# Attention in pairs of heads: both heads' scores on two row halves, values stationary, probabilities scaled on ScalarE

## The chip, the cores and the metric

One NeuronCore of one Trainium2 chip runs the whole program. The metric is device time in microseconds, from runs of the whole kernel: 657.15 us is the median of three (657.02 to 658.48).

## The reference

One layer on 256 tokens of width 1024, all in float32: a feed-forward block, a mixer of a convolution branch and an attention branch, and a second feed-forward block. What matters here is the attention. There are 16 heads of 64, and with 256 tokens there is one block of 256 keys, so that only the causal part of the head's own block is left:

```
s_own = jnp.einsum('bhqd,bhkd->bhqk', q_c, k_own).astype(jnp.float32) * scale
s_own = jnp.where(k_pos[None, :] <= q_pos[:, None], s_own, NEG_INF)
...
p = jax.nn.softmax(logits, axis=-1)
...
o = (jnp.einsum('bhqk,bhkd->bhqd', p_own, v_own.astype(jnp.float32))
...
y_b = moba_attention(q, k, v) @ w_attn_proj
```

## The kernel before

Every large product is made of three: a float32 weight is split into a high part (`hi`, rounded on ScalarE, L91) and a low part (`lo`, on VectorE or GpSimd, L93), and the activations likewise. `gemm` (L97) goes through the weights in pieces of two k-tiles of 128 rows by 512 columns; a piece is loaded (SyncE's queue), split, and used by twelve matmuls of 512 columns (two token tiles, two k-tiles, L133 to L135). Five pieces can be in flight.

The attention is a generator of small steps. While the keys, queries and values of heads 8 to 15 and then the four gate products run, `gemm` takes steps from it after each piece: `SIDE` of them, 1.25 in the first three products (12 pieces) and 1.5 in the four gate products (16 pieces). Beside it runs the convolution, in steps of two 255-column multiply-adds on VectorE (L317), by `PUMP` per piece. A scheduler orders each engine's instructions by a simulated timeline, so that the order in the trace is near that of the source, but not the same.

`score(h)` makes the scores of one head for two token tiles t (the first sees 128 keys, the second 256), as two matmuls with 64 rows, rows 0 to 63 for even heads and 64 to 127 for odd ones (L419). VectorE adds the mask and takes the maximum (L430), negates it (L434), and ScalarE takes Exp with row sums (L437). `value(h)`, one score later, transposes the three 128x128 blocks of probabilities (L448), copies them to SBUF (L452), and multiplies with the transposed probabilities as the stationary operand and 64 columns of v moving (L459). VectorE takes the reciprocals of the row sums (L465) and scales the output with them (L466). After each four heads the output is transposed by `to_T` (L472, L178) and split into its parts `oh` and `ol` (L187, L188) for the product with `w_attn`.

A float32 matmul stands in the trace as two passes of a weight load and a matmul; a transpose and a product of the split weights as one. PSUM tiles `tr` have three buffers.

Of the kernel before, what the change touches and what calls it, by code (L numbers as in the profile page):

```python
# [17 lines left out]
P = 128  # L18
S = 256
# [10 lines left out]

# columns of the packed small parameters
C_GM, C_G2, C_QN, C_KN = 0, 8, 16, 17
C_CB, C_LG, C_LB, C_DW = 18, 26, 34, 42
C_ALL = C_DW + KD * TAPS

KP = 2            # k-tiles of 128 rows in one piece of weights
RAW_BUFS, HI_BUFS, LO_BUFS = 5, 5, 5
B8_BUFS = 13
SIDE = 1.25, 1.5   # steps of the attention per piece of weights
PUMP = 3, 3.5, 3, 8   # steps of the convolution per piece of weights  # L40
WARM = 8          # products that only bring the tensor engine to its full clock
LATER = 2         # pieces of the next product before the transposes of the last


class Build:
# [9 lines left out]

# [1 line left out]
    def big(self, name, dt=F32):  # L57
# [7 lines left out]

# [1 line left out]
    def pump(self, n=1):  # L67
# [19 lines left out]

# [1 line left out]
    def split(self, raw, hi, lo, pool_lo):  # L89
# [7 lines left out]
    def gemm(self, w, c, n, kt, ah, al, pump=0, pool=0.0, first=False, split_k=None,  # L97
             side=None, before=None):
        """acc[t][128 tokens, n] = A @ W[:, chunk c]; ah/al give the [128, 128]
        stationary parts of A^T for (k, t)."""  # L100
        nc = self.nc
# [45 lines left out]

# [1 line left out]
    def rsqrt_mean(self, ss, n, width):  # L149
        """(ss / n + eps) ** -0.5 for a [128, width] tile"""  # L150
        nc = self.nc
        ms = self.tmp.tile([P, width], F32, tag=f"ms{width}", name="ms", bufs=2)
        nc.vector.tensor_scalar(ms, ss, 1.0 / n, EPS, ALU.mult, ALU.add)  # L153
        r = self.tmp.tile([P, width], F32, tag=f"rs{width}", name="rs", bufs=4)
        nc.gpsimd.tensor_tensor(r, ms, self.neghalf[:, :width], ALU.pow)  # L155
        return r

    def sum_squares(self, x, ss, t, c):
        """ss[:, c, t] = sum of squares of x[t][:, chunk c]"""
        junk = self.tmp.tile([P, CH], F32, tag="junk", name="junk", bufs=2)  # L160
        self.nc.scalar.activation(
            junk, x[:, t * D + c * CH : t * D + (c + 1) * CH], AF.Square,
            accum_out=ss[:, c * 2 + t : c * 2 + t + 1],
        )
# [6 lines left out]
    def to_T(self, src, hi, lo, k0, gain=None):  # L171
        """src(t, j) -> [128 tokens, 128 columns] for two column tiles j; writes
        the transposed tiles k0, k0 + 1 of hi/lo ([128, k, 256])."""
        nc = self.nc
        ps = self.tr()
        for j in range(2):
            for t in range(2):
                nc.tensor.transpose(  # L178
                    ps[:, j * S + t * P : j * S + (t + 1) * P], src(t, j), self.ident
                )  # L180
        return self.split_T(ps, hi, lo, k0, 2, gain)
# [28 lines left out]

# [1 line left out]
    def ffn(self, wgu, wd, hT, rstd_of, x, emit, tail=None, before=None, after=None):  # L212
        """emit(t, c, psum) takes the down products of chunk c."""
        nc = self.nc
# [68 lines left out]
    def residual_T(self, x_new, ss, hi, lo, gain):  # L283
        """after chunk c of the new residual stream: statistics, transposed parts"""
        def transp(c):
# [11 lines left out]

# [1 line left out]
    def conv(self, uT, tiles):  # L299
        """replaces tile c of uT ([channels, tokens]) by its convolution"""  # L300
        nc = self.nc
# [65 lines left out]

# [1 line left out]
    def head_norm(self, acc, rstd, c, dst, gain):  # L369
        """normalises the 8 heads of chunk c and writes them transposed"""  # L370
        nc = self.nc
# [36 lines left out]
    def attention(self, qT, kT, v, oh, ol):  # L408
        nc = self.nc
        scale = HD ** -0.5  # L410
        sums = {}
        probs = {}

        def score(h):
            b, r = h // 2, slice((h % 2) * HD, (h % 2 + 1) * HD)
            sums[h] = self.tmp.tile([P, 2], F32, tag="sums", name="sums", bufs=3)
            ps = self.tr()
            for t in range(2):
                nc.tensor.matmul(  # L419
                    ps[:, t * P : t * P + (t + 1) * P],  # L420
                    qT[r, b * S + t * P : b * S + (t + 1) * P],
                    kT[r, b * S : b * S + (t + 1) * P],
                    start=True, stop=True,
                )
            pr = self.tmp.tile([P, 3 * P], F32, tag="pr", name="pr", bufs=3)
            mx = self.tmp.tile([P, 2], F32, tag="mx", name="mx", bufs=3)
            nb = self.tmp.tile([P, 2], F32, tag="nb", name="nb", bufs=3)
            for t in range(2):
                sl = slice(t * P, t * P + (t + 1) * P)
                nc.vector.tensor_tensor_reduce(  # L430
                    pr[:, sl], ps[:, sl], self.mask[:, (1 - t) * P :], 1.0, NEG,
                    ALU.add, ALU.max, mx[:, t : t + 1],
                )
            self.anchor = nc.vector.tensor_scalar(nb, mx, -scale, None, ALU.mult)  # L434
            for t in range(2):
                sl = slice(t * P, t * P + (t + 1) * P)
                nc.scalar.activation(  # L437
                    pr[:, sl], pr[:, sl], AF.Exp, bias=nb[:, t : t + 1], scale=scale,
                    accum_out=sums[h][:, t : t + 1],
                )  # L440
            probs[h] = pr

        def value(h):
            pr = probs.pop(h)
            g = h // 4
            ps = self.tr()
            for i in range(3):
                nc.tensor.transpose(  # L448
                    ps[:, i * P : (i + 1) * P], pr[:, i * P : (i + 1) * P], self.ident
                )  # L450
            pT = self.tmp.tile([P, 3 * P], F32, tag="pT", name="pT", bufs=2)
            nc.scalar.copy(pT, ps[:, : 3 * P])  # L452
            if h % 4 == 0:
                self.on = self.tmp.tile([P, CH], F32, tag="on", name="on", bufs=2)
            on = self.on
            for t in range(2):
                o = ps[:, 3 * P + t * HD : 3 * P + (t + 1) * HD]
                for kt in range(t + 1):
                    nc.tensor.matmul(  # L459
                        o, pT[:, (t + kt) * P : (t + kt + 1) * P],  # L460
                        v[:, kt * D + h * HD : kt * D + (h + 1) * HD],
                        start=kt == 0, stop=kt == t,
                    )
            rs = self.tmp.tile([P, 2], F32, tag="rsum", name="rsum", bufs=2)
            nc.vector.reciprocal(rs, sums.pop(h))  # L465
            nc.vector.tensor_tensor(  # L466
                on.rearrange("p (t h d) -> p t h d", t=2, d=HD)[:, :, h % 4, :],
                ps[:, 3 * P :].rearrange("p (t d) -> p t d", d=HD),
                rs.unsqueeze(2).to_broadcast((P, 2, HD)), ALU.mult,
            )  # L470
            if h % 4 == 3:
                self.last_att = self.to_T(  # L472
                    lambda t, q: on[:, t * S + q * P : t * S + (q + 1) * P], oh, ol, g * 2
                )

        for h in range(H + 1):
            if h < H:
                score(h)
                yield 1
            if h > 0:  # L480
                value(h - 1)
                yield 1

# [1 line left out]
    def run(self):  # L485
# [31 lines left out]
        def start(k0):  # L517
            """the part of x^T that goes with the weights from k-tile k0 on"""
            if k0 == 0:
# [34 lines left out]
        def rstd_x():  # L554
            """statistics of x by products of its squares with ones"""
            sums = self.tr()
# [14 lines left out]

        # FFN 1
        x1 = self.big("x1")
# [15 lines left out]

        # mixer  # L590
        w_in = w_of("w_in", KD)
# [117 lines left out]

        # FFN 2  # L710
        out = io["out"]
# [17 lines left out]
def _pack(cols, kt):  # L729
    """list of [K, n] column chunks -> one flat array, each chunk [128, k, n]"""  # L730
    return np.concatenate(
# [66 lines left out]
```

## Time and profile before

| what | value |
|---|---|
| median of 3 runs | 657.15 us (657.02 to 658.48) |
| span of the profiled execution | 655.4 us |
| TensorE (PE) busy | 645.9 us, 99% |
| VectorE (DVE) busy | 417.5 us, 64% |
| ScalarE (ACT) busy | 332.9 us, 51% |
| GpSimd (POOL) busy | 133.3 us, 20% |
| attention's first scores, last values | 282.0 us, 406 us from the span's start |

The span is that of one profiled execution, from its first to its last instruction. A busy time is the union of an engine's instructions; matmuls overlap one another, so that PE's says only that something was in flight. Start times in the timeline say more. The idle time of an engine counts only where it is the one that others wait for.

### The profile page before, as it was taken

The numbers are of one execution on the slowest core, as the hardware profiler recorded it, in microseconds if no ns is written. First come the engines' busy times: TensorE is split into PE (matmuls) and PEld (weight loads), VectorE is DVE, ScalarE is ACT, GpSimd is POOL, SyncE is SP. The second block draws the span as 40 slices with busy tenths as digits, with TensorE's granted clock in tenths as the row PEclk, the third lists the DMA queues.
The fourth block names the chain that finished last, engine by engine and source line by source line (L and its number), as shares of the span: only waits on it lengthen the run. The fifth ranks groups of instructions, "written<-read, shape, count | busy, mean of one in ns | idle before, by whom it ended". The sixth has DMA issues, their size and how long they took to land.

```text
span 655.4 us, 8241 instructions
## 1 busy us (share of the span) xinstructions
PE 645.9 (99%) x3004; PEld 528.7 (81%) x3004; DVE 417.5 (64%) x692; ACT 332.9 (51%) x476; POOL 133.3 (20%) x80
## 2 busy tenths in 40 slices
PE   7999999999999999999999999999999999999997
PEld 5788888888888888877778778788888888888886
DVE  6765645464622599999999685675754646455541
ACT  6544455353545546666465374943745535444330
POOL 6200000000035667947545300000000000000000
PEclk8999999999999999999999999999999999999999
DMA  8864655556554545435333442265645555546630
GB/s 279 324 211 161 212 172 194 192 160 225 175 192 148 210 176 194 162 137 174 131 137 135 154 135 92 92 230 174 207 161 197 188 198 170 199 161 191 216 124 32
DMA packets 33000, 114.98 MB, mean 175 GB/s; under 512 B 3648, under 2 KB 5056, under 8 KB 32960
## 3 DMA queue, kind: packets, MB, share of 16 engines
q1 hardware_dynamic: 32960, 114.46, 51.3%
q8 instruction: 23, 0.38, 0.2%
q14 instruction: 17, 0.14, 0.1%
HBM read 113.40 MB, written 1.05 MB: 175 GB/s over the span
## 4 chain that ended last, share of the span: by engine, by line
PE 84%; DVE 9%; ACT 3%; issue 1%; DMA 1%; SPq 0%; DVEq 0%; ACTq 0%
PE acc L133 26%; PE acc L134 26%; PE acc L135 26%; DVE cv L317 5%; PE tr L178 2%; DVE lo L93 1%; DMA raw<-w1gu 1%; PE tr L419 1%; PE tr L459 1%; DVE hxn L385 1%; ACT gate L670 1%; DVE nb L434 1%; ACT z L359 1%; PE tr L448 1%; DVE pr L430 0%
## 5 line engine op out<-in xcount | busy, mean ns | idle before, releaser
L91 ACT CAST hi<-raw 128x1024 fp32r<-128x1024 f32 (+1 forms) x216 | 223.1, 1037 | 241.7 <-PE acc L135 214.3
L93 DVE TENSOR_TENSOR lo<-raw,hi 128x1024 fp32r<-128x1024 f32 (+1 forms) x174 | 215.9, 1245 | 183.3 <-ACT hi L91 178.3
L93 POOL TENSOR_TENSOR lo<-raw,hi 128x1024 fp32r<-128x1024 f32 x42 | 101.5, 2434 | 220.8 <-ACT hi L91 220.7
L317 DVE SCALAR_TENSOR_TENSOR cv<-uT,cst,cv 128x255 f32<-128x255 f32 (+14 forms) x240 | 95.2, 463 | 0.0
L134 PE MATMUL acc<-lo,h1h 128*128 128x512 f32 x224 | 88.0, 393 | 0.0
L135 PE MATMUL acc<-hi,h1l 128*128 128x512 f32 x224 | 87.8, 395 | 0.0
L133 PE MATMUL acc<-hi,h1h 128*128 128x512 f32 x224 | 87.7, 397 | 0.0
L133 PE MATMUL acc<-hi,hTh 128*128 128x512 f32 x176 | 68.8, 397 | 2.2 <-ACT hi L91 2.2
L134 PE MATMUL acc<-lo,hTh 128*128 128x512 f32 x176 | 69.9, 397 | 0.6 <-DVE lo L93 0.6
L135 PE MATMUL acc<-hi,hTl 128*128 128x512 f32 x176 | 69.2, 394 | 0.0
L133 PE MATMUL acc<-hi,h2h 128*128 128x512 f32 x176 | 69.1, 393 | 0.0
L133 PE MATMUL acc<-hi,aTh 128*128 128x512 f32 x176 | 68.7, 391 | 0.0
L135 PE MATMUL acc<-hi,aTl 128*128 128x512 f32 x176 | 68.5, 389 | 0.0
L134 PE MATMUL acc<-lo,aTh 128*128 128x512 f32 x176 | 68.5, 389 | 0.0
L134 PE MATMUL acc<-lo,h2h 128*128 128x512 f32 x176 | 68.4, 390 | 0.0
L135 PE MATMUL acc<-hi,h2l 128*128 128x512 f32 x176 | 67.2, 390 | 0.0
L133 PEld LDWEIGHTS acc<-hi,h1h 128*128 128x128 f32 x224 | 42.1, 188 | 10.2 <-issue 1.7
L135 PEld LDWEIGHTS acc<-hi,h1l 128*128 128x128 f32 x224 | 42.1, 188 | 9.0 <-issue 0.7
L134 PEld LDWEIGHTS acc<-lo,h1h 128*128 128x128 f32 x224 | 42.1, 188 | 8.5 <-issue 0.3
L133 PEld LDWEIGHTS acc<-hi,hTh 128*128 128x128 f32 x176 | 33.4, 191 | 9.6 <-ACT hi L91 2.9
L134 PEld LDWEIGHTS acc<-lo,hTh 128*128 128x128 f32 x176 | 33.4, 190 | 8.8 <-DVE lo L93 2.1
L155 POOL TENSOR_TENSOR rs<-ms,neghalf 128x8 f32<-128x8 f32 (+2 forms) x13 | 17.3, 1332 | 111.5 <-DVE ms L153 111.3
(133 smaller groups left out, 800.9 us busy)
## 6 DMA issues: line engine op xcount, KB each, us to landing
raw<-w_in SPq DMA_DIRECT2D x56, 512.0 KB, 3.2
raw<-w2gu SPq DMA_DIRECT2D x44, 512.0 KB, 4.2
raw<-w1gu SPq DMA_DIRECT2D x43, 512.0 KB, 5.2
raw<-w1d SPq DMA_DIRECT2D x22, 512.0 KB, 4.4
raw<-w2d SPq DMA_DIRECT2D x22, 512.0 KB, 4.4
raw<-w_attn SPq DMA_DIRECT2D x8, 512.0 KB, 3.2
raw<-w_conv SPq DMA_DIRECT2D x8, 512.0 KB, 3.2
raw<-w_out SPq DMA_DIRECT2D x8, 512.0 KB, 4.9
```

The lines of the kernel that those rows point to most:

```text
L91: nc.scalar.copy(hi, raw)
L93: ins = eng.tensor_tensor(lo, raw, hi.bitcast(F32), ALU.subtract)
L133: nc.tensor.matmul(o, ah(k, t), wh, start=st, stop=False)
L134: nc.tensor.matmul(o, ah(k, t), wl, start=False, stop=False)
L135: nc.tensor.matmul(o, al(k, t), wh, start=False, stop=sp)
L155: nc.gpsimd.tensor_tensor(r, ms, self.neghalf[:, :width], ALU.pow)
L178: nc.tensor.transpose(ps[:, j * S + t * P : j * S + (t + 1) * P], src(t, j), self.ident)
L317: nc.vector.scalar_tensor_tensor(o, i, w, o, ALU.mult, ALU.add)
L359: nc.scalar.activation(z[:, q * S : (q + 1) * S], ps[:, q * S : (q + 1) * S], AF.Silu, bias=cst[:, C_LB + c + q : C_LB + c + q + 1], scale ...
L385: nc.vector.tensor_tensor(xn.rearrange("p (h d) -> p h d", d=HD), x.rearrange("p (h d) -> p h d", d=HD), r.unsqueeze(2).to_broadcast((P, 8 ...
L419: nc.tensor.matmul(ps[:, t * P : t * P + (t + 1) * P], qT[r, b * S + t * P : b * S + (t + 1) * P], kT[r, b * S : b * S + (t + 1) * P], sta ...
L434: self.anchor = nc.vector.tensor_scalar(nb, mx, -scale, None, ALU.mult)
```

## The change

The generator now takes a pair of heads b (heads 2b and 2b + 1) in three steps: `score(b)`, `flip(b)` and `value(b)`. `SIDE` becomes 1.0, 1.0.

- `score` issues four matmuls, alternating between the heads and so between rows 0 to 63 and 64 to 127, into two `tr` tiles. Masking, Exp and row sums are as before, on tiles of twice the width with two buffers in place of three. The reciprocals follow at once, and ScalarE multiplies the probabilities by them in place.
- `flip` transposes the six blocks of the pair.
- `value` takes 64 columns of v as the stationary operand and moves the transposed probabilities (256 columns for the first key tile, 128 for the second). The first head's output lands on partitions 0 to 63 and the second's on 64 to 127 of one `tr` tile, already transposed, and is split into `oh` and `ol` per pair. `to_T` is no longer called for the attention.

```diff
-SIDE = 1.25, 1.5   # steps of the attention per piece of weights
+SIDE = 1.0, 1.0
...
-        def score(h):
-            b, r = h // 2, slice((h % 2) * HD, (h % 2 + 1) * HD)
...
+        def blk(q, t):
+            o = q * 3 * P + t * P
+            return slice(o, o + (t + 1) * P)
+
+        def score(b):
+            ps = [self.tr(), self.tr()]
+            for t in range(2):
+                for q in range(2):
+                    r = slice(q * HD, (q + 1) * HD)
+                    nc.tensor.matmul(
+                        ps[q][:, t * P : t * P + (t + 1) * P],
+                        qT[r, b * S + t * P : b * S + (t + 1) * P],
+                        kT[r, b * S : b * S + (t + 1) * P],
+                        start=True, stop=True,
+                    )
+            pr = self.tmp.tile([P, 6 * P], F32, tag="pr", name="pr", bufs=2)
...
+            for q in range(2):
+                for t in range(2):
+                    i = q * 2 + t
+                    nc.vector.tensor_tensor_reduce(
+                        pr[:, blk(q, t)], ps[q][:, t * P : t * P + (t + 1) * P],
+                        self.mask[:, (1 - t) * P :], 1.0, NEG,
+                        ALU.add, ALU.max, mx[:, i : i + 1],
+                    )
+            self.anchor = nc.vector.tensor_scalar(nb, mx, -scale, None, ALU.mult)
+            for q in range(2):
+                for t in range(2):
+                    i = q * 2 + t
+                    nc.scalar.activation(
+                        pr[:, blk(q, t)], pr[:, blk(q, t)], AF.Exp, bias=nb[:, i : i + 1],
+                        scale=scale, accum_out=sums[:, i : i + 1],
+                    )
+            rs = self.tmp.tile([P, 4], F32, tag="rsum", name="rsum", bufs=2)
+            nc.vector.reciprocal(rs, sums)
+            for q in range(2):
+                for t in range(2):
+                    i = q * 2 + t
+                    nc.scalar.activation(
+                        pr[:, blk(q, t)], pr[:, blk(q, t)], AF.Copy, scale=rs[:, i : i + 1]
+                    )
+            state[b] = pr
+
+        def flip(b):
+            pr = state[b]
+            pT = self.tmp.tile([P, 6 * P], F32, tag="pT", name="pT", bufs=2)
+            for q in range(2):
+                ps = self.tr()
+                for i in range(3):
+                    o = (q * 3 + i) * P
+                    nc.tensor.transpose(
+                        ps[:, i * P : (i + 1) * P], pr[:, o : o + P], self.ident
+                    )
+                nc.scalar.copy(pT[:, q * 3 * P : (q + 1) * 3 * P], ps[:, : 3 * P])
+            state[b] = pT
+
+        def value(b):
+            pT = state.pop(b)
             ps = self.tr()
...
+            for kt in range(2):
+                for q in range(2):
+                    h = b * 2 + q
+                    o = q * 3 * P + kt * 2 * P
+                    n = (2 - kt) * P
                     nc.tensor.matmul(
-                        o, pT[:, (t + kt) * P : (t + kt + 1) * P],
+                        ps[q * HD : (q + 1) * HD, kt * P : S],
                         v[:, kt * D + h * HD : kt * D + (h + 1) * HD],
-                        start=kt == 0, stop=kt == t,
+                        pT[:, o : o + n],
+                        start=kt == 0, stop=kt == 1, skip_group_check=True,
                     )
...
-            nc.vector.reciprocal(rs, sums.pop(h))
-            nc.vector.tensor_tensor(
-                on.rearrange("p (t h d) -> p t h d", t=2, d=HD)[:, :, h % 4, :],
-                ps[:, 3 * P :].rearrange("p (t d) -> p t d", d=HD),
-                rs.unsqueeze(2).to_broadcast((P, 2, HD)), ALU.mult,
-            )
-            if h % 4 == 3:
-                self.last_att = self.to_T(
-                    lambda t, q: on[:, t * S + q * P : t * S + (q + 1) * P], oh, ol, g * 2
-                )
+            self.last_att = self.split_T(ps, oh, ol, b, 1, None)
...
+        NB = H // 2
+        for b in range(NB + 1):
+            if b < NB:
+                score(b)
                 yield 1
+            if b > 0:
+                flip(b - 1)
+                yield 1
+                value(b - 1)
+                yield 1
```

## Rows read from the trace of the kernel before

**Rows 1.** The page's first part: busy time, share of the span, instructions.
```profile
PE 645.9 (99%) x3004; PEld 528.7 (81%) x3004; DVE 417.5 (64%) x692; ACT 332.9 (51%) x476; POOL 133.3 (20%) x80
```

**Rows 2.** The chain that ended last: shares of the span by engine.
```profile
PE 84%; DVE 9%; ACT 3%; issue 1%; DMA 1%; SPq 0%; DVEq 0%; ACTq 0%
```

**Rows 3.** Waits of PE, largest two kinds: us in total, times, longest us.
```profile
PE acc L133 <- ACT hi L91: 2.2, 1, 2.2
PE tr L510 <- DVE ones L515: 1.1, 1, 1.1
...
```

**Rows 4.** Timeline of PE, 281 to 283 us: start us, us, instruction.
```profile
281.72 0.39 PE L133 MATMUL acc<-hi,h1h 128*128 128x512 f32 x1
282.04 0.93 PE L419 MATMUL tr<-kT,qT 64*128 64x128 f32 x8
...
283.23 0.39 PE L134 MATMUL acc<-lo,h1h 128*128 128x512 f32 x1
```

**Rows 5.** Timeline of PE, 296 to 301 us.
```profile
296.18 0.39 PE L134 MATMUL acc<-lo,h1h 128*128 128x512 f32 x1
...
296.86 0.39 PE L134 MATMUL acc<-lo,h1h 128*128 128x512 f32 x1
297.18 0.92 PE L419 MATMUL tr<-kT,qT 64*128 64x128 f32 x4
...
298.36 0.39 PE L134 MATMUL acc<-lo,h1h 128*128 128x512 f32 x1
298.59 0.39 PE L135 MATMUL acc<-hi,h1l 128*128 128x512 f32 x1
298.82 1.45 PE L459 MATMUL tr<-v,pT 128*128 128x64 f32 x12
...
300.39 0.39 PE L134 MATMUL acc<-lo,h1h 128*128 128x512 f32 x1
```

**Rows 6.** Timeline of PE, 348 to 350 us.
```profile
348.92 0.39 PE L135 MATMUL acc<-hi,h1l 128*128 128x512 f32 x1
349.15 0.49 PE L448 MATMUL tr<-ident,pr 128*128 128x128 f32 x3
...
349.71 0.39 PE L134 MATMUL acc<-lo,h1h 128*128 128x512 f32 x1
```

**Rows 7.** Timeline of PE in short windows: starts of three of one head's passes.
```profile
344.30 0.49 PE L419 MATMUL tr<-kT,qT 64*128 64x128 f32 x2
344.41 0.59 PE L419 MATMUL tr<-kT,qT 64*128 64x256 f32 x2
344.63 0.38 PE L419 MATMUL tr<-kT,qT 64*128 64x256 f32 x1
```

**Rows 8.** Two stretches: length, busy PE PEld DVE ACT POOL, PEclk, DMA share, GB/s.
```profile
268.00:345.00 77.00, 75.91 (x375) 60.05 (x373) 77.00 (x200) 45.75 (x88) 47.21 (x22) 1.00 0.41 149
345.00:406.00 61.00, 60.83 (x317) 48.47 (x316) 46.23 (x128) 33.60 (x70) 15.38 (x8) 1.00 0.38 134
```

**Rows 9.** Groups of DVE by form: busy us, mean ns, idle before.
```profile
L434 DVE TENSOR_SCALAR nb<-mx 128x2 f32<-128x2 f32 x16 | 8.6, 537 | 0.2
...
L466 DVE TENSOR_TENSOR on<-tr,rsum 128x128 f32<-128x128 f32 x16 | 4.6, 286 | 6.3 <-PE tr L459 6.3
...
L188 DVE TENSOR_TENSOR ol<-tr,oh 128x512 fp32r<-128x512 f32 x4 | 2.7, 683 | 1.2 <-ACT oh L187 1.1
...
L465 DVE RECIPROCAL rsum<-sums 128x2 f32<-128x2 f32 x16 | 2.5, 154 | 0.9 <-ACT pr L437 0.7
```

**Rows 10.** Groups of ACT by form, 268 to 406 us.
```profile
L437 ACT ACTIVATE pr<-pr,nb 128x256 f32<-128x256 f32 x16 | 7.9, 494 | 0.0
...
L437 ACT ACTIVATE pr<-pr,nb 128x128 f32<-128x128 f32 x16 | 6.4, 401 | 29.0 <-DVE nb L434 29.0
```

**Rows 11.** Waits of ACT, 268 to 406 us: us in total, times, longest us.
```profile
ACT pr L437 <- DVE nb L434: 29.0, 10, 5.9
ACT hi L91 <- PE acc L135: 13.3, 10, 4.0
```

More of the change, by code (lines that the diff above doesn't have):

```diff
@@ L410, in attention @@
         scale = HD ** -0.5
-        sums = {}
-        probs = {}
-        def score(h):
-            b, r = h // 2, slice((h % 2) * HD, (h % 2 + 1) * HD)
-            sums[h] = self.tmp.tile([P, 2], F32, tag="sums", name="sums", bufs=3)
-            ps = self.tr()
[L418 to L423, printed above, removed]
-                )
[L425 to L432, printed above, removed]
-                )
[L434 to L458, printed above, removed]
+        state = {}
@@ new lines, in blk @@
+        def blk(q, t):
[13 more added lines that the diff above has]
+            pr = self.tmp.tile([P, 6 * P], F32, tag="pr", name="pr", bufs=2)
+            mx = self.tmp.tile([P, 4], F32, tag="mx", name="mx", bufs=2)
+            nb = self.tmp.tile([P, 4], F32, tag="nb", name="nb", bufs=2)
+            sums = self.tmp.tile([P, 4], F32, tag="sums", name="sums", bufs=2)
+            for q in range(2):
[23 more added lines that the diff above has]
+            state[b] = pr
@@ L464, in value @@
-            rs = self.tmp.tile([P, 2], F32, tag="rsum", name="rsum", bufs=2)
-            nc.vector.reciprocal(rs, sums.pop(h))
-            nc.vector.tensor_tensor(
-                on.rearrange("p (t h d) -> p t h d", t=2, d=HD)[:, :, h % 4, :],
-                ps[:, 3 * P :].rearrange("p (t d) -> p t d", d=HD),
-                rs.unsqueeze(2).to_broadcast((P, 2, HD)), ALU.mult,
-            )
-            if h % 4 == 3:
-                self.last_att = self.to_T(
-                    lambda t, q: on[:, t * S + q * P : t * S + (q + 1) * P], oh, ol, g * 2
-                )
@@ L476, in attention @@
-        for h in range(H + 1):
-            if h < H:
-                score(h)
+                        pT[:, o : o + n],
+                        start=kt == 0, stop=kt == 1, skip_group_check=True,
+                    )
+            self.last_att = self.split_T(ps, oh, ol, b, 1, None)
[3 more added lines that the diff above has]
+                score(b)
                 yield 1
-            if h > 0:
-                value(h - 1)
+            if b > 0:
+                flip(b - 1)
+                yield 1
+                value(b - 1)
```

## Prediction

> **What bounds the kernel now.** I read the page's first part, then the chain of waits, then TensorE's own waits. TensorE (PE) is busy 99% of the span [rows 1], the chain that ended last lies on it for 84% [rows 2], and its waits are small: the longest is 2.2 us at the start, and the eight kinds add up to 5.4 us [rows 3]. So an edit is worth what it takes off PE's stream, provided that no other engine then holds PE up. A busy PE row hides how dense the stream is, since its matmuls overlap; I therefore price by start times in the timeline. Two stretches of the mixer hold the attention, and in both the granted clock is 1.00 [rows 8]. VectorE (DVE) is the engine to watch: 77.00 of 77.00 us busy from 268 to 345, but 46.23 of 61.00 after that. ScalarE (ACT) is busy 45.75 and 33.60.
>
> **Prices on PE.** Large products start 0.227 us apart: 296.18 to 296.86 is three of them [rows 5]. A visit to something small costs the time from the product before it to the second product after it, less 2 x 0.227.
> - Scores of one head: 296.86 to 298.36 is 1.50, less 0.45: 1.05 us. Its four passes stream only 0.66 (0.11 for 128 columns and 0.22 for 256, twice each, [rows 7]); 0.39 is spent getting in and out of the 64-row form.
> - Scores of two heads side by side: once in this trace heads 0 and 1 happened to run next to each other, eight passes: 281.72 to 283.23 [rows 4], 1.51 less 0.45: 1.06 us. The second head, on the other 64 rows, was almost free. That is the row on which the forecast rests.
> - Values of two heads, twelve passes: 298.59 to 300.39, 1.80 less 0.45: 1.35, or 0.675 a head [rows 5].
> - Three transposes: 348.92 to 349.71, 0.79 less 0.45: 0.34, or 0.11 each [rows 6].
>
> **The change part by part.**
> - *Scores in pairs.* Before: 14 visits of one head and one of two, 14 x 1.05 + 1.06 = 15.8. After: 8 visits of two, 8 x 1.06 = 8.5. PE -7.3.
> - *Values stationary.* Before 16 x 0.675 = 10.8. After, each pair has eight passes, four on each 64-column half of the array, and moves 256 and 128 columns as the scores do. No row of before shows two column halves. Nearest is the pair of row halves: 8 x 1.06 = 8.5, PE -2.3. If the halves run one after the other, a pair streams 2 x 0.66 and pays 0.39 to get in and out: 1.71 x 8 = 13.7, PE +2.9. I take -2.3, because the same machine in the same two-pass form overlapped two halves fully; both ends go into the range.
> - *Output born transposed.* Four calls of the transposing helper go, with 16 transposes: 16 x 0.11 = 1.8. PE -1.8. The 48 transposes of probabilities stay, six together in place of three.
> - *DVE.* Gone: 16 multiplications by the reciprocals (4.6), 8 of 16 reciprocals (1.2), 8 of 16 negations (half of 8.6 = 4.3; at least 1.2 if each cost only what a reciprocal of that size does). Evictions of the low part: 4 of 512 columns (2.7) become 8 of 256; between the 0.286 of 128 columns and the 0.683 of 512 a line gives about 0.42 for 256, so 3.3, +0.6 [rows 9]. Sum -9.5 (ends -6.4 and -9.5).
> - *ACT.* 32 scalings of probabilities are new, in the forms of the Exp rows: 16 x (0.494 + 0.401) = 14.3 [rows 10]. The high part's evictions also double in count; at 0.494 each they are at most 4.0 in all.
> - *New waits.* The reciprocal on DVE now waits for four Exps of its pair; convolution products and low parts of weights are queued behind it. The scalings on ACT wait for that reciprocal; behind them are casts of weights, for which PE waits. PE's transposes wait for the scalings; large products are behind them. Cover: a pair's transposes are issued four steps after its scores, about four pieces of weights of 12 x 0.227 = 2.7 us, some 11 us, against 1.06 of scores, 1.8 each of Exp and of scaling [rows 10], and DVE's masking in between. If the cover goes, PE loses the difference. I cost this at nothing of its own.
> - *Steps.* 32 steps at 1.25 and 1.5 per piece become 24 at 1.0: both end at piece 24 of 28. The scores of heads 8 and 9 now come one piece (2.7 us) after the transposes that make their queries; four transposes (0.45) and one eviction, at up to 0.7 by the nearest row of that width [rows 9], fit in that. If not, PE waits about 1.
> - *Queues.* No DMA is added or moved, and POOL's and SP's queues keep their work.
> - *What is late next: DVE.* About half of the attention lies in the stretch where DVE has no idle time. There PE gets shorter by half of 11.4 = 5.7 and DVE by half of 9.5 = 4.7, so PE would run into DVE for 1.0 (ends 0, if DVE's backlog goes into its 14.8 us idle later, and 5.7, all of that half). I take 1.0.
>
> Sum: -7.3 - 2.3 - 1.8 + 1.0 = -10.4. The profiled span is 655.4 and the median of the runs 657.15, so 1.75 lies around the span or between executions; I keep it. 655.4 - 10.4 = 645.0, and 646.8 as time.
>
> **A rule against the change.** The scores' 1.05 us hold 0.39 that is not streaming [rows 5, 7]. The Trainium skill, "TensorEngine Tiling (Array Packing)", section Key Properties, says that changing the tiling mode drains the TensorE. By that rule the trace agrees at the scores, and the values, until now in full 128x128 form, would start to pay it too; my 1.06 a pair has it in. Were there no drain, the pair would cost 0.66 and the sum would be 3.2 lower.
>
> **The rivals.**
> 1. *Column halves don't overlap.* For it: no row of before shows them. Against: the row halves. -7.3 + 2.9 - 1.8 + 1.0 = -5.2: 652.0.
> 2. *Passes start strictly in the order written.* The change writes one head's matmul, of two passes, and then the other's; only the second pass of one would then overlap the first of the next: 0.11 + 0.11 + 0.22 + 0.22 + 0.22 = 0.88 of streaming in place of 0.66 for a pair, 0.22 more in each of 16 visits, +3.5: 650.3. Against: 281.72 to 283.23 was full overlap [rows 4]; there the source has one head's four passes before the other's, and such an order would have overlapped only 0.11 of 2 x 0.66. The Trainium skill, "TensorE: Matmul & The Clock Gate", section The mechanism, says that matmuls are strictly first in, first out and only weight loads overtake. By that rule this rival holds; the trace's one pair speaks against it.
> 3. *The pairs are broken up.* The kernel's scheduler orders instructions by its own timeline and may put transposes between a pair's scores. Then -7.3 goes: -3.1, 654.0. Against: it laid two separate heads side by side unasked [rows 4].
> 4. *ACT becomes the bound (slower).* ACT is busy 79.4 of the 138 us and waits 29.0 for the negated maxima, in ten stops of 2.9 [rows 8, 11]. After: 79.4 + 14.3 = 93.7 in 127.6, or 33.9 idle. Each pair now stops ACT twice, once for the maxima and once for the reciprocals, 16 stops. It decides at 33.9 / 16 = 2.1 us a stop. At 2.9 it overflows by 12.5, to 659.3, and with the evictions' 4.0 to 663; middle 661. For it: DVE's full stretch, through which the reciprocal must pass. Against: 13.3 us of ACT's idle time today is waiting for PE to free a buffer [rows 11], which says that casts run well ahead, and DVE is slack in the second half.
>
> **How the numbers follow.** Forecast 0.60; rival 1 0.16; rival 2 0.08; rival 3 0.04; rival 4 0.12. Faster by over 0.3% (which is about what a measurement of this kernel can tell from no change) means under 655.2: all of the first four, 0.88, less 0.02 for stalls of rival 4's kind that only cancel the gain. Of rival 4 I give 0.09 to slower and the rest to same: 0.86, 0.05, 0.09. Range: the low end is the sum without the 1.0, with PE's 1.26 us of idle time in the two stretches [rows 8] gone and 0.1 less per value visit for half-wide weights: -11.4 - 1.26 - 0.8 = -13.46: 643.7. The high end takes in rivals 1 to 3 and 1.0 of ACT's stops on rival 3: 655.0. It leaves out rival 4 and little else.
>
> **What would show it.** Right: scores in 8 groups of eight passes at about 0.86 us from first start to next product; value groups of eight passes at the same; no transposes of the attention's output; from 268 to the end of the gates some 10 us shorter, PE still 99% busy. Wrong: value groups at 1.3 or more (rival 1) or both groups near 1.1 (rival 2); scores in groups of four (rival 3); PE idle behind casts, with ACT waiting on reciprocals over 2.1 us a stop (rival 4).

## The result and the profile after

The changed kernel takes 653.47 us (median of four runs, 653.23 to 653.98) against 657.82 for the kernel before, run beside it: a ratio of 0.9939 [0.9927, 0.9952], 4.35 us or 0.6% faster. That lies inside the range, but 10.4 us were forecast. The profiled span fell from 655.4 to 652.2 us, 3.2; the profile after lost 0.75 us in its first stage, at products that the change doesn't touch, so that the change itself is worth 4.0 in the profile.

The page of the kernel after: first part, and the chain that ended last (answer to [rows 1, 2]).

```profile
PE 640.5 (98%) x2956; PEld 519.8 (80%) x2956; DVE 413.1 (63%) x664; ACT 342.6 (53%) x512; POOL 132.5 (20%) x80
...
PE 90%; DVE 3%; ACT 3%; DMA 1%; issue 1%; SPq 0%; DVEq 0%; ACTq 0%
```

PE bounds the kernel more than before (90% of the chain). What holds it up, by PE's waits of the kernel after (us in total, times, longest; answer to [rows 3]):

```profile
PE acc L133 <- ACT hi L91: 2.9, 1, 2.9
PE acc L133 <- ACT u2h L365: 1.3, 1, 1.3
PE tr L466 <- DVE ms L153: 1.2, 1, 1.2
```

The first is at the start of the kernel. The second has grown (it was 0.2), and is behind the attention: the first product with `w_conv` waits for the rounded output of the convolution branch (`u2h`). The third is in the attention, at 316.54: transposes wait for VectorE. The kernel before had about as much of that in its attention, in three stops:

```profile
PE tr L178 <- DVE on L466: 0.6, 1, 0.6
...
PE tr L397 <- DVE mx L430: 0.3, 1, 0.3
...
PE tr L178 <- DVE mx L430: 0.2, 1, 0.2
```

The rest of the gain has to be looked for in PE's stream. One pair runs there as forecast: the values of one pair and, right behind, the scores of another (PE, kernel after: start us, us, instruction; answer to [rows 4, 5]).

```profile
340.81 0.39 PE L135 MATMUL acc<-hi,h1l 128*128 128x512 f32 x1
341.13 0.87 PE L481 MATMUL tr<-pT,v 128*64 128x256 f32 x8
341.93 0.93 PE L423 MATMUL tr<-kT,qT 64*128 64x128 f32 x8
342.79 0.50 PE L133 MATMUL acc<-hi,h1h 128*128 128x512 f32 x1
343.13 0.40 PE L134 MATMUL acc<-lo,h1h 128*128 128x512 f32 x1
```

Sixteen passes go between 340.81 and 343.13, which by the prediction's measure (less 2 x 0.227) is 1.87 us for both groups, even below the 2 x 1.06 that it had. The eight value passes take 0.80 from their first start to the scores' first. The more frequent picture, in the same view:

```profile
354.68 0.40 PE L133 MATMUL acc<-hi,h1h 128*128 128x512 f32 x1
355.01 0.65 PE L481 MATMUL tr<-pT,v 128*64 128x256 f32 x2
355.58 0.92 PE L423 MATMUL tr<-kT,qT 64*128 64x128 f32 x4
356.43 0.86 PE L481 MATMUL tr<-pT,v 128*64 128x256 f32 x6
357.23 0.92 PE L423 MATMUL tr<-kT,qT 64*128 64x128 f32 x4
358.08 0.50 PE L133 MATMUL acc<-hi,h1h 128*128 128x512 f32 x1
358.41 0.40 PE L134 MATMUL acc<-lo,h1h 128*128 128x512 f32 x1
```

The same sixteen passes, but cut: the first head's first value matmul (two passes), the scores of one head (four), the other six value passes, the scores of the other head. Nothing lies beside its partner, and the array changes its form five times in place of three. From the product before to the second product after it is 3.28 us by the same measure, 1.41 more. In the whole trace only two of eight value groups are whole (341.13 and 396.68), and only two of eight pairs of scores (282.78 and 341.93), with a third partly so (306.18). Added up place by place against whole groups (waits taken out, and 0.11 for each transpose that stands between), this costs 9.2 us: 1.4 here, and 0.8 to 1.9 at six other places. It is rival 3.

### The profile page after: what moved, and what is told of

Read it like the earlier page. It is cut to its first block, busy times and chain, and to the rows that moved or that the text cites. A ratio compares the mean times of both kernels' runs of the same rounds, so it can differ in the third digit from the quotient of the medians.

```text
span 652.2 us, 8131 instructions
## 1 busy us (share of the span) xinstructions
PE 640.5 (98%) x2956; PEld 519.8 (80%) x2956; DVE 413.1 (63%) x664; ACT 342.6 (53%) x512; POOL 132.5 (20%) x80
## 3 DMA queue, kind: packets, MB, share of 16 engines
HBM read 113.40 MB, written 1.05 MB: 175 GB/s over the span
## 4 chain that ended last, share of the span: by engine, by line
PE 90%; DVE 3%; ACT 3%; DMA 1%; issue 1%; SPq 0%; DVEq 0%; ACTq 0%
PE acc L134 28%; PE acc L133 28%; PE acc L135 28%; PE tr L178 2%; PE tr L423 1%; DMA raw<-w1gu 1%; PE tr L481 1%; DVE cv L317 1%; DVE lo L93 1%; ACT hi L91 1%; PE tr L466 1%; ACT gate L686 1%; ACT pr L445 0%; DVE hxn L385 0%; PE tr L397 0%
## 5 line engine op out<-in xcount | busy, mean ns | idle before, releaser
L317 DVE SCALAR_TENSOR_TENSOR cv<-uT,cst,cv 128x255 f32<-128x255 f32 (+26 forms) x240 | 94.4, 463 | 0.1
L133 PEld LDWEIGHTS acc<-hi,h1h 128*128 128x128 f32 x224 | 42.1, 188 | 10.4 <-issue 1.3
```

Source lines behind the costliest of these rows:

```text
L133: nc.tensor.matmul(o, ah(k, t), wh, start=st, stop=False)
L317: nc.vector.scalar_tensor_tensor(o, i, w, o, ALU.mult, ALU.add)
```

## The experiments

Of the two theories on record, A says that the gain went where the groups are cut, and B that it went into ScalarE's scalings and the waits around them. Runs of the kernel before beside the experiments had medians of 657.09 to 657.56. Where I give a difference in the attention alone, PE's large products of two profiles were matched by their number, and their starts compared from just before the first scores on; by this measure the change as made is 5.3 ahead of the kernel before at the end of the `w_attn` product, and 4.0 ahead at the end of the `w_conv` product.

**One line: the second half first.** The value matmuls need the transposed probabilities of two heads, which ScalarE copies in two instructions, first head first. If the first matmul in the text needs only the first copy, the scheduler can place it, and finds something else for the time until the second copy. In `value`, the loop runs the other way here, so that the first matmul needs the copy that comes last.

```diff
             for kt in range(2):
-                for q in range(2):
+                for q in (1, 0):
```

> The changed kernel with one edit: value() issues the matmul of the second head of the pair ahead of the first one's, so that its first matmul waits for the copy of probabilities that ends last, and all four can then follow one another. Theory A (the pairs of products are broken up on TensorE, each broken pair costing 0.9 to 1.6 us, some 7.7 us in all by the timeline of the changed kernel; one score pair breaks newly, 1.0): about 6.7 us faster than the change, 646 to 648. Theory B (the gain went into waits for VectorE and ScalarE): nothing changes there, 652.5 to 654.5.

Measured: 649.41 us (648.89 to 650.92), ratio 0.9887 [0.9872, 0.9902]: 4.1 faster than the change as made, and 3.5 faster than the control below, which ran beside it. PE, kernel with the line swapped:

```profile
354.88 0.39 PE L133 MATMUL acc<-hi,h1h 128*128 128x512 f32 x1
355.20 0.87 PE L481 MATMUL tr<-pT,v 128*64 128x256 f32 x8
356.00 0.93 PE L423 MATMUL tr<-kT,qT 64*128 64x128 f32 x8
356.86 0.50 PE L134 MATMUL acc<-lo,h1h 128*128 128x512 f32 x1
```

The pair that was cut at 355.01 is whole. All eight value groups are whole now, and six of eight pairs of scores; at the end of `w_attn` PE is 9.55 ahead of the kernel before, 4.2 more than in the change. The scores and values alone got 6.4 shorter by the count above; PE's waits up to there grew from 1.5 to 3.7, mostly by a new one of 2.1 for VectorE's masking. Arithmetic and data are the same: the order of a loop of two is worth 3.5 to 4.1 us.

**The control: the same swap in the scores.** In `score`, both matmuls become ready together, so that the order should not matter.

```diff
             for t in range(2):
-                for q in range(2):
+                for q in (1, 0):
```

> Control to the first: the same swap of heads in score() alone. The products of value() stay broken as in the change. Theory A: as the change, 652.5 to 654.5. If the swap itself (and not the unbroken group) were what helps, this would be faster too.

Measured: 652.93 (652.73 to 653.63), 0.9939 [0.9924, 0.9953]: as the change, and the same value groups are cut (353.88, 367.37 and 374.12 among them). So not any reordering helps, but the one of the values.

**Whole groups without the scalings.** The row sums' division is left out of the computation here: the 32 multiplications on ScalarE are gone.

```diff
-            for q in range(2):
-                for t in range(2):
-                    i = q * 2 + t
-                    nc.scalar.activation(
-                        pr[:, blk(q, t)], pr[:, blk(q, t)], AF.Copy, scale=rs[:, i : i + 1]
-                    )
```

> The first experiment without the 32 scalings of probabilities on ScalarE (the row sums' division is left out of the computation; the reciprocals stay). It takes 14.4 us off ScalarE. Theory A: TensorE's stream is the same, within 1 us of the first experiment. Theory B (ScalarE's longer queue holds TensorE up): 3 us or more faster than the first.

Measured: 646.26 (646.2 to 646.38), 0.9836 [0.9819, 0.9852]; 3.15 below the swapped kernel. A expected at most 1, so B has a share: once the groups are whole, the scalings cost 3.2 us. Where they cost it shows in PE's waits, first with the scalings (swapped kernel), then without (the ones at the kernel's start, for splitting weights and in its last stages are left out).

```profile
PE tr L397 <- DVE mx L436: 2.1, 1, 2.1
PE acc L133 <- ACT u2h L365: 1.3, 1, 1.3
...
PE tr L423 <- ACT ynat L331: 0.8, 1, 0.8
PE tr L481 <- ACT pT L469: 0.6, 1, 0.6
```

```profile
PE tr L397 <- DVE mx L436: 0.3, 1, 0.3
PE acc L133 <- ACT u2h L365: 0.3, 1, 0.3
PE tr L328 <- ACT uT L320: 0.2, 1, 0.2
PE tr L475 <- ACT pT L463: 0.2, 1, 0.2
```

The four waits of the attention and of its end add up to 4.8 with the scalings, and the four without to 1.0. Without them PE is 11.6 ahead of the kernel before at the end of `w_attn` and 11.5 at the end of `w_conv`, so that almost nothing is given back on the way. That it is so near the prediction's sum without its 1.0 for DVE, 11.4, is in part chance: two pairs of scores are still cut here (286.18 and 335.34), and whole groups cost less than the prediction had them at.

**The end of the attention.** What is given back between the ends of `w_attn` and `w_conv` (1.4 in the change, 1.5 with the swapped line) is ScalarE's. Its stream in the kernel after, from the last rounding of the attention's output:

```profile
403.85 0.37 ACT L187 CAST oh<-tr 128x256 fp32r<-128x256 f32 x1 [4.92 <-PE tr L481]
404.24 1.28 ACT L686 ACT_TABLE_LOAD   x1
405.53 4.28 ACT L686 ACTIVATE gate<-gate 128x512 f32<-128x512 f32 x8
409.81 1.28 ACT L359 ACT_TABLE_LOAD   x1
411.11 1.93 ACT L359 ACTIVATE z<-tr,cst 128x256 f32<-128x256 f32 x4
412.92 2.00 ACT L91 CAST hi<-raw 128x1024 fp32r<-128x1024 f32 x2
414.80 1.16 ACT L365 CAST u2h<-z 128x512 fp32r<-128x512 f32 x2
```

The gates' Sigmoids, two loads of function tables, the convolution's Silus and the rounding for `w_conv` form a chain of 11.0 us behind the attention's last output. In the kernel before it took 10.2, from 407.41 to 417.64, and without the scalings 10.0, from 396.45 to 406.47; in these two, one cast of weights (1.05 us) stands ahead of `u2h`, in the change and in the swapped kernel two (2.00), and PE waits 0.2 and 0.3 in place of 1.3. An attention that ends earlier on PE meets a chain that doesn't get shorter, and gets a cast longer here. In the step that makes Silus and roundings two tiles at a time, I ordered each pair's Silus behind the rounding of the pair before:

```diff
-            nc.scalar.copy(h, z)
+            after = nc.scalar.copy(h, z)
```

> The first experiment (value halves swapped) with one edit in the convolution's last step: ScalarE makes the rounded part of one pair of tiles before the Silu of the next pair. In the change and in the first experiment ScalarE did four Silus and two weight casts ahead of it, and TensorE waited 1.3 us for the first product of w_conv; in the kernel before it alternated. If the loss of 1.4 to 1.5 us there comes from that order: about 1.4 us faster than the first experiment. If ScalarE is simply late because of the 32 scalings: no change.

Measured: 650.2 (649.82 to 652.97), 0.9901 [0.9879, 0.9922], no gain over 649.41. PE's wait for `u2h` fell from 1.3 to 0.4, and a wait of 0.9 for the rounded activations of a later product came in its place. That chain is real; this is not the way to shorten it.

**The scalings on another engine.** On VectorE (`nc.vector.tensor_scalar` in place of `nc.scalar.activation`, on the swapped kernel):

> The first experiment with the 32 scalings of probabilities on VectorE in place of ScalarE. Leaving them out gave 3.2 us (third experiment). If it is ScalarE's queue that costs those 3.2 us: 646 to 648, near the third. If any engine in the chain from scores to transposes would cost as much, or VectorE's full stretch takes it back: 649 to 652.

Measured: 667.19 (666.64 to 667.28), 1.0148 [1.0133, 1.0163]: a miss for every expectation. PE's waits:

```profile
PE tr L466 <- DVE ol L188: 7.7, 3, 3.1
```

PE can't start transposes, since no `tr` buffer is free, and the buffer waits for VectorE's `ol`. So the prediction's eye on VectorE was not empty: the scalings there turn the gain into a loss of 10. On GpSimd (`nc.gpsimd.tensor_scalar`):

> As the sixth, with the scalings on GpSimd, which was busy 62 of 138 us in the two stretches. By ScalarE's queue: near the third experiment, 646 to 648. If GpSimd's own time (0.9 us for 128x256 in the start of this kernel, some 3 us a pair) or its conflict with VectorE's small operations counts: 649 to 655.

Measured: 652.35 with a scatter of 649.92 to 656.12 over eight runs, 0.9927 [0.9903, 0.9951]: not better than ScalarE, and no more can be said.

**The scores' term alone.** The kernel before with the paired `score` only; values, division and transposes as they were; one step per piece.

```diff
-SIDE = 1.25, 1.5   # steps of the attention per piece of weights
+SIDE = 1.0, 1.0   # steps of the attention per piece of weights
...
-        def score(h):
+        def score(b):
+            ps = [self.tr(), self.tr()]
```

> The kernel before with the change's score() alone, in three steps a pair (scores of the pair, value of one head, value of the other), SIDE 1.0; values, scaling of the output and its transposes as before. With three PSUM buffers the scheduler keeps only 2 of 8 score pairs side by side here, two more are split by transposes only. By the prediction's term (-7.3 for scores in pairs): 650. By theory A (a pair costs what its pieces cost when something comes between): about 2 us faster than before or less, 655 to 657.

Measured: 658.63 (656.94 to 659.06, ten runs), 1.0015 [1.0005, 1.0025]: no gain, where the prediction's -7.3 would have given 650. Two of eight pairs run side by side, the other twelve heads alone, as two of them do at 360.09 and 361.30 with two transposes between. By the prediction's own prices that is 12 x 1.05 + 2 x 1.06 = 14.7 in place of 15.8: -1.1. Against it stands a new wait of PE, 1.9 us in one stop, for a buffer that VectorE's scaling has to leave:

```profile
PE tr L419 <- DVE on L469: 1.9, 1, 1.9
```

**Pairing in the text against pairing on PE.** The swapped kernel, but with the scores of each head written on their own (and `SIDE` 1.25, 1.5, so that the steps end at the same piece):

```diff
-        def score(b):
-            ps = [self.tr(), self.tr()]
+        def score(h):
+            b, q = h // 2, h % 2
+            ps = self.tr()
...
-                score(b)
+                score(2 * b)
+                yield 1
+                score(2 * b + 1)
```

> The first experiment with score() per head again (two tiles of the kernel before in place of one of a pair, SIDE 1.25, 1.5), values and scaling as in the first experiment. The scheduler lays 5 of 8 pairs of scores side by side by itself, against 6 of 8 in the first experiment. Theory A (only what is adjacent on TensorE counts, not how the source pairs it): within 1.5 us of the first experiment, 649 to 651. If pairing in the source is what brings the 7.3 us: about 656.

Measured: 650.18 (649.24 to 650.66), 0.989 [0.9875, 0.9905], within 0.8 of the paired text. The scheduler laid five of the eight pairs side by side unasked. So it's not how the matmuls are written that counts, but what stands next to them on PE.

**A fourth `tr` buffer.** A pair of scores needs two free `tr` tiles of three at once, and in the swapped kernel the two pairs that are still cut (286.34 and 343.55) could be waiting for the second. To make room for a fourth, the convolution's two accumulators share one tile:

```diff
-        return self.ps.tile([P, CH], F32, tag="tr", name="tr", bufs=3)
+        return self.ps.tile([P, CH], F32, tag="tr", name="tr", bufs=4)
...
-            accs = [self.ps.tile([P, S], F32, tag="cv", name="cv", bufs=2) for _ in range(2)]
+            cv = self.ps.tile([P, 2 * S], F32, tag="cv", name="cv", bufs=1)
+            accs = [cv[:, :S], cv[:, S:]]
```

> The first experiment with a fourth PSUM buffer for scores and transposes (the convolution's two accumulators share one bank for it), so that the two tiles of a score pair are free together and nearly all score pairs stay whole as well. Theory A: two more broken pairs at 1.05 us gone, about 2 us faster than the first, 644 to 646, unless the convolution's shared tile delays its end. Theory B: as the first.

Measured: 671.23 (670.68 to 673.22), 1.0221 [1.0204, 1.0238]: a miss in time, but all eight value groups and all eight pairs of scores run side by side (one pair in two visits of two passes a head), which speaks for the buffers. The time went to the convolution: with one tile for both accumulators it ended at 423.9 us, not 378, and PE stood still for it, from 411 on. PE's longest wait, and two stretches (length, busy PE PEld DVE ACT POOL, PEclk, DMA share, GB/s):

```profile
PE tr L329 <- ACT uT L321: 13.4, 1, 13.4
```

```profile
415.00:420.00 5.00, 0.00 (x0) 0.00 (x0) 4.74 (x9) 0.00 (x0) 0.00 (x0) 0.61 0.93 316
420.00:425.00 5.00, 0.59 (x3) 0.60 (x4) 3.67 (x8) 0.65 (x2) 0.00 (x0) 0.50 0.01 3
```

**Moving the steps.** Four runs sought the 3.2 us by pace. Fewer steps of the convolution in the first stretch (swapped kernel, `PUMP` from 3, 3.5, 3, 8 to 3, 3, 4, 8):

> The first experiment with PUMP 3, 3, 4, 8: fewer steps of the convolution per piece while keys, queries and values are made, more in the gates, where VectorE had 15 us idle; same order of groups on TensorE. If TensorE's 2.1 us wait for a score's masking on VectorE is due to VectorE's full first stretch: 1 to 2 us faster than the first, 647 to 648.5. If not: no change.

Measured: 652.35 (651.93 to 653.1), 0.9925 [0.9908, 0.9941], 2.9 worse. The wait of 2.1 at L397 went, as expected; one of 2.5 came at L328 for the same cause (masking on VectorE late), and the one for `u2h` grew to 2.0. Behind that the granted clock fell, too:

```profile
410.00:415.00 5.00, 2.11 (x8) 1.41 (x8) 4.50 (x5) 5.00 (x7) 0.00 (x0) 0.96 0.43 129
415.00:420.00 5.00, 5.00 (x17) 3.96 (x17) 4.43 (x6) 4.21 (x8) 0.00 (x0) 0.70 0.79 251
```

The same with the attention later and then faster (`SIDE` 0.75, 1.25):

> As the tenth, with SIDE 0.75, 1.25: the attention's steps are spread more thinly over the stretch in which VectorE is full. One score pair fewer is broken (7 of 8 whole), worth 1.05 us by theory A: 646 to 648, if the end of the attention does not come too late for ScalarE's Sigmoids and Silus behind it; then 649 to 651.

Measured: 653.06 (651.85 to 654.21), 0.9935 [0.992, 0.995]; PE waited 4.0 us for the copies of transposed probabilities. And the swapped kernel with the attention ending earlier (`SIDE` 1.0, 1.5), to give ScalarE's chain a head start; with the scalings, and without (the division left out again):

> The first experiment with SIDE 1.0, 1.5: the same groups on TensorE up to the sixth pair, but the attention's last values come some 70 large products (16 us) earlier. Theory: in the change and the first experiment ScalarE needs 11 us from the attention's last rounding over eight Sigmoids, two table loads and the Silus to the first operand of w_conv, and TensorE gets there 1.4 to 1.6 us too early; with the attention's end moved ahead that wait is gone: 647 to 648.5. If the wait has another cause: no change, 649 to 650.

> As the twelfth, without the 32 scalings (the row sums' division is left out of the computation). In the third experiment, leaving them out was worth 3.2 us, of which 1.5 was the wait for the first operand of w_conv. With that wait gone in both: 1.5 to 2 us faster than the twelfth, 645 to 646.5. If the scalings cost 3 us wherever the attention ends: 644 to 645.

Measured: 656.96 (654.52 to 658.66, ten runs), 0.9992 [0.998, 1.0004], and 651.36 (651.04 to 651.78), 0.9908 [0.9893, 0.9923]: both misses, 7.6 and 5.1 worse than the same kernels at 1.0, 1.0. The last output of the attention did come earlier (393.87, not 399.45), but with the scalings the Silus started later, at 414.88 and not 406.71. The convolution's normalization had moved back (its last step on VectorE from 394.61 to 406.15), and the transposes that feed the Silus with it. PE waited for the Silus:

```profile
PE tr L352 <- ACT z L359: 2.5, 1, 2.5
```

Without the scalings PE waited 2.3 there as well, so that this wait is not theirs; between these two runs they cost 5.6 us, more than the 3.2 above. So the last 3 us are not free for a different pace: each run traded one wait for another. The swapped kernel, 649.41, is the fastest here that computes the whole, and beats both kernels.

## Why the prediction went wrong

**The step that failed** is "After: 8 visits of two, 8 x 1.06". The price was right, the count was not: it supposes that what the text pairs stays together on PE. By the prediction's prices the attention's groups were to cost 8.5 + 8.5 = 17.0, from 15.8 + 10.8 = 26.6, 9.6 less. Whole groups that follow each other would be cheaper still: 1.06 for each of the first two pairs of scores, six times 1.87 for values with scores behind them, and 0.95 for each of the last two groups of values (396.68), 15.2. With 9.2 for the cuts they cost 24.4. Counted the same way they cost 28.2 in the kernel before, since transposes stood inside some of its groups too (290.29 to 291.90, for one). So this part gave 3.8 in place of 9.6, and with the transposes' 1.8 that is 5.6, against 5.3 seen at the end of `w_attn`, up to which PE's waits are nearly the same in both kernels (1.3 and 1.5). After the chain's loss 4.0 are left.

**Rival 3** had the mechanism and, at 654.0, nearly the time, but a chance of 0.04. The nearness is in part luck: it gave up all that the scores were to gain and left the values whole, while in the trace both were cut and both kept a part. Against it stood that the scheduler had laid two heads side by side unasked [rows 4]. That row was one of fifteen visits, the other fourteen were single: it showed that two heads can overlap, and was read as showing that they would. The prediction also cut only the scores; the values were cut as well, six groups of eight, each behind the first head's first matmul. That the swap of this one order mends the values is shown; that the scheduler cuts there because ScalarE copies the two heads' probabilities one after the other is inferred. Before the cut at 355.01 both copies had been done for a microsecond (ACT, kernel after):

```profile
353.13 0.83 ACT L469 COPY pT<-tr 128x384 f32<-128x384 f32 x2
```

No wait on the chip asked for that cut: it stands in the order that the scheduler wrote. For the scores, the run with four buffers points to the second free `tr` tile, but it moved the convolution too; no run here has the fourth buffer alone.

**What held.** *Column halves overlap* (the unknown that was bounded from -2.3 to +2.9): eight passes in 0.80 us, below the 0.86 that it asked for. Rival 1 (1.3 or more) falls, and so does rival 2 (near 1.1 for both groups). The Trainium skill, "TensorE: Matmul & The Clock Gate", section The mechanism, has matmuls start strictly first in, first out. By the prediction's working that would be 0.88 of streaming for a pair; at 341.13 the group was through in 0.80, and here the measurement decides. (In what order the passes stand in PE's own instruction stream, no trace here shows.) *The transposes of the output* are gone, and PE's group holds the 48 of the probabilities. *ScalarE's and VectorE's prices* held; by form, 265 to 425 us (busy us, mean ns, idle before; answer to [rows 9, 10]):

```profile
L454 ACT ACTIVATE pr<-pr,rsum 128x256 f32<-128x256 f32 x16 | 8.0, 501 | 0.0
...
L454 ACT ACTIVATE pr<-pr,rsum 128x128 f32<-128x128 f32 x16 | 6.4, 399 | 0.0
```

```profile
L441 DVE TENSOR_SCALAR nb<-mx 128x4 f32<-128x4 f32 x8 | 3.5, 442 | 0.1
L188 DVE TENSOR_TENSOR ol<-tr,oh 128x256 fp32r<-128x256 f32 x8 | 3.4, 420 | 6.7 <-ACT oh L187 6.7
```

The scalings are 14.4 (forecast 14.3), the low parts 3.4 (3.3), the negations 3.5 (4.3).

**Rival 4** (ScalarE the bound) did not come in the change: it needed 2.1 us in each of 16 stops. ScalarE had 13.9 in six, all for the negated maxima, and none for the reciprocals (waits of ACT, 265 to 425 us; answer to [rows 11]):

```profile
ACT pr L445 <- DVE nb L441: 13.9, 6, 5.3
```

But "I cost this at nothing of its own" was not right either. With whole groups the scalings cost 3.2 us. The cover of 11 us that the prediction counted out was there for the transposes; the longest new wait, 2.1 at L397, was for a `tr` buffer, by the releaser that the profile names because the masking was late. What the scalings cost in the change as made, where the groups are cut, no run here shows.

**What is late next** was named as VectorE, for 1.0 us: "PE would run into DVE". PE did wait 1.2 for VectorE in one stop, but hardly longer than in the three stops of the kernel before (1.1), and VectorE had room in the first stretch (71.48 of 74.00; it was 77.00 of 77.00 in [rows 8]):

```profile
268.00:342.00 74.00, 72.75 (x353) 55.93 (x351) 71.48 (x176) 50.37 (x104) 47.24 (x22) 1.00 0.48 155
```

What was new was ScalarE's chain behind the attention, for 1.3. The size was near, the place was another, and that the size was near is luck. The range held because its upper end took in rival 3.

## What to carry to other kernels

Pairs that gain by running side by side are worth what their neighbours on the engine allow: find in the trace of before how many of them are adjacent, and price the change for both cases. What was seen once in fifteen visits is a case that can happen, not yet the one to expect. Write first the operation whose input comes last, so that a group of matmuls becomes ready all at once and nothing can be put between; this was worth nearly as much as the whole change (3.5 to 4.1 us, against 4.35). When work on the bounding engine gets shorter, follow the chain of the next stage back through the other engines, since it starts at the same last output and doesn't shrink.

## What the runs showed of the hardware

Float32 passes with 64 stationary columns on the two column halves overlap as those on two row halves do: eight value passes in 0.80 us, where one head's four score passes alone hold PE for 0.85 (355.58 to 356.43). Going into a half-array form and out again shows at each change: 0.32 and 0.33 from a product to the first small pass (340.81 to 341.13, 354.68 to 355.01) and 0.34 between the first two products after (342.79 to 343.13), against 0.227 from product to product. The Trainium skill, "TensorEngine Tiling (Array Packing)", section Key Properties, says that a change of the tiling mode drains the TensorE. The trace agrees in that going in and out costs at each place above, and five changes of form in place of three, without the overlap, made 3.28 us out of 1.87.

The granted clock fell behind a gap in PE's work. In the kernel with less convolution early it was 0.70 as a mean of 415 to 420, after 2.11 busy of 5.00 us, and 17 matmuls fall into those 5 us, where 24 fall into the next: the late input was paid for a second time. In the kernel with four buffers it was 0.61 from 415 to 420, in which no matmul ran, and 0.50, the lower of the two levels (1.2 of 2.4 GHz), from 420 to 425.
